# Moving the sums of the other rows behind the last expert's last bias, and one activation part ahead of one weight part, at the end of a mixture-of-experts kernel

## The chip, the cores and the metric

The kernel runs on one core of a Trainium2 chip. The metric is the device time of one execution in microseconds; lower is better. The core has a matrix engine (PE, whose weight loads are listed as PEld), a vector engine (DVE), an activation engine (ACT), a general engine (POOL) and a queue engine (SP) that here only issues transfers. Each engine takes its instructions strictly in the order in which the program lists them for it, so an instruction that waits holds back everything that is listed behind it on the same engine.

## The reference

One layer over 512 latent tokens of width 1024: a modulated norm, a mixer (a chunked scan with a convolution, and a pooling group), an output projection, a second modulated norm, a router that takes the best 4 of 32 experts for each token, the experts, and a last norm. Only the end matters here:

```
hb  = x_pad[toks] @ w1[e] + b1[e]
act = min(hb[::2], 7) * sigmoid(1.702 * min(hb[::2], 7)) * (clip(hb[1::2], -7, 7) + 1)
y   = (act @ w2[e] + b2[e]) * gate
x   = x + g2 * sum of y over the token's four experts
out = x * rsqrt(mean(x * x) + 1e-6) * final_norm_w
```

All inputs are 32-bit floats. The last line needs the complete sum of a token's row, so no row of the output can be made before the last expert that the row uses has been added.

## The kernel before, in words

Every 32-bit product is made of parts: an operand is split into a high part, which ACT copies out in a reduced format (fp32r), and a low part, which DVE makes by subtraction. PE then multiplies the pairs that matter and adds them up in its accumulators.

The 32 experts are worked one after the other, sorted by how many tokens they have. The late positions of the order, and the last one among them, have room for 64 tokens (the case `m == LT` in the code; `LT = 64`). For these the high and low activations lie side by side as one 128-column operand, so that the low products come out in the lower 64 accumulator rows; `rest` (L1321) copies those rows by ACT into the lower half of `b2h`, and the bias product `bias2` (L1339) adds them to the upper ones together with the bias.

The second layer of an expert reads its weights in four pieces of 1 MB, `kk` = 0 to 3 (L1672). Each piece is split by `split` (L1088): the high part on ACT (L1093), the low part on DVE (L1094). There are three pairs of buffers for high and low parts, so a piece waits until PE is done with the piece three before it. PE multiplies the activations with them in `prod` (L1347, matmuls on L1353), eight matmuls to a piece for the last expert. The activations come from `transposed` (L1122): PE transposes, ACT copies the high part (L1129), DVE subtracts the low part (L1130).

When an expert is done, `finish` (L1370) multiplies its rows by gate and `g2` (two DVE instructions, L1374) and adds them to `acc_scr`, an array in HBM, by an indirect transfer that POOL issues (L1376). The last expert's rows are not waited for in that way. Its output rows are added on chip instead: the four 128-row chunks of `acc_scr`, without the last expert, are read back by four transfers of 512 KB (L1683, `tot`), after the scatter of the expert before it has landed. The function `others` (L1685) brings one chunk into PE's accumulators, by a product with the identity: chunk 0 whole in 32 bits (`WHOLE = (0,)`; PE runs it in two passes for each half, which the trace lists as four matmuls), chunks 1 to 3 as a high part (ACT, L1690) and a low part (POOL for 1 and 3, DVE for 2, L1693), four matmuls each (L1697). Then the last expert's rows (`y`, split into `yh` by ACT on L1708 and `yl` by DVE on L1709) are put to their tokens by products with a 0/1 matrix `place` (L1716), 16 matmuls that contract over 64 rows only, four to a chunk and in the order of the chunks. From the finished sums ACT takes squares (L1728), DVE and POOL make the factor (L1730, L1731), DVE scales (L1734), and SP writes the chunk out (L1735).

In the program text the chunks 0 to 2 of `others` stand behind the four pieces and before `rest`, `bias2` and `finish`; chunk 3 stands behind `yh` and `yl` (`LATE_HI = 1`), and its high part is also held behind the last `yh` on ACT.

The order of the instructions on each engine is not the order of the text. A planner walks through the program with its own costs for each operation and lists, for each engine, what by its reckoning is ready first, the earlier in the text ahead where several are. `after(i, j, why)` (L1386) puts an instruction `i` behind `j`, in that list, without a semaphore where both are on one engine.

Of the kernel before, what the change touches and what calls it, by code (L numbers as in the profile page):

```python
# [5 lines left out]
F32 = mybir.dt.float32  # L6
# [5 lines left out]
ALU = mybir.AluOpType  # L12
# [9 lines left out]
NT = T // P  # L22
# [12 lines left out]
E = 32  # L35
# [62 lines left out]
def mixer_and_moe(tc, a):  # L98
    nc = tc.nc
    SC, VE, PO, PE, SP = nc.scalar, nc.vector, nc.gpsimd, nc.tensor, nc.sync  # L100
# [135 lines left out]
    for k in range(KT):  # L236
        for h in range(2):
            r = raw_tile([P, D])
            wdma = SP.dma_start(r, wm[:, k, h * D:(h + 1) * D])
            hi, lo = split_weights(r, [P, D])  # L240
            for i, w in enumerate((hi, lo)):
                for j in range(2):
                    last = PE.matmul(modp[2 * h + j][0:4, :], lhsT=sil4[:, k, :], rhs=w[:, j * T:(j + 1) * T],
                                     start=(k == 0 and i == 0), stop=(k == KT - 1 and i == 1))
            with tc.issue_after(wdma.ins):
                if 2 * k + h in (5, 9):
                    j = k // 2 - 1
# [4 lines left out]
    ahead = []  # L252
# [22 lines left out]
    then = [[(con[:, P:], con_src[:, P:])], [scan_con], [pool_con, (pw, a["pool_w"].rearrange("o g i f -> i (o g) f"))]]  # L275
# [13 lines left out]
    for j in range(16):  # L289
# [8 lines left out]
                            op0=ALU.add, op1=ALU.mult)  # L298
# [11 lines left out]
    for lo, n, which, oh_, ol_ in ((NT, NTC, 1, hch, hcl), (0, NT, 0, hxh, hxl)):  # L310
        for k in range(KT):
            tp = bank("S")
            w = n * P
            for j in range(n):
# [3 lines left out]
                             op0=ALU.mult, op1=ALU.add)  # L318
            SC.activation(row_of(oh_, k), val[:, 0:w], AF.Copy)
            (PO if k % 3 == 2 else VE).tensor_tensor(row_of(ol_, k), val[:, 0:w], row_of(oh_, k).bitcast(F32),  # L320
                                                     op=ALU.subtract)
# [166 lines left out]
    for xh_, xl_, n, off in ((hch, hcl, TC, T), (hxh, hxl, T, 0)):  # L488
        dps = bank("S")
        o = dps[0:2 * H, 0:n]  # L490
# [210 lines left out]
    sums = {}  # L701
# [104 lines left out]
    for pr in range(2):  # L806
        cath, catl = cat[pr]
        for k2 in range(6):
            tp = bank("S")
            for i in range(2):  # L810
                kk = 2 * k2 + i
# [3 lines left out]
            for i in range(2):  # L815
                kk = 2 * k2 + i
# [4 lines left out]
                                        op0=ALU.mult, op1=ALU.subtract)  # L821
# [220 lines left out]
    b2h = pc.tile([P, D], F32R, name="b2h")  # L1042
# [19 lines left out]
    newest_lo = [None]  # L1062
    loads = [0]
    own = [(strm, SR)]
    ring = [(pcat, RC)] * 3 + [(strm, SR)] * SR + [(pcat, RC)] * (RC - 3)
# [50 lines left out]
    def gather(t, col, m):  # L1116
# [2 lines left out]
                              bounds_check=T - 1, oob_is_err=False)  # L1119
        return t  # L1120

    def transposed(src, m, pool, name, bufs, tbank):  # L1122
        if m == LT:
            both = pool.tile([P, KT, 2, LT], F32R, name=name + "h", tag=name + "h", bufs=bufs)
            tp = tbank()
            for k in range(KT):
                PE.transpose(tp[:, k * LT:(k + 1) * LT], src[0:LT, k * P:(k + 1) * P], ident[0:LT, 0:LT])  # L1127
            v = tp.rearrange("p (k t) -> p k t", k=KT)
            SC.activation(both[:, :, 0, :], v, AF.Copy)  # L1129
            VE.tensor_tensor(both[:, :, 1, :], v, both[:, :, 0, :].bitcast(F32), op=ALU.subtract)  # L1130
            return (both.rearrange("p k i t -> p k (i t)"),)
        hi = pool.tile([P, KT, P], F32R, name=name + "h", tag=name + "h", bufs=bufs)
        lo = pool.tile([P, KT, P], F32R, name=name + "l", tag=name + "l", bufs=bufs)
        for h in range(2):
            tp = tbank()
            for k in range(4):
                PE.transpose(tp[:, k * P:k * P + m], src[0:m, (h * 4 + k) * P:(h * 4 + k + 1) * P],
                             ident[0:m, 0:m])
            o = hi[:, h * 4:(h + 1) * 4, 0:m]
            v = tp.rearrange("p (k t) -> p k t", k=4)[:, :, 0:m]  # L1140
            SC.activation(o, v, AF.Copy)
            VE.tensor_tensor(lo[:, h * 4:(h + 1) * 4, 0:m], v, o.bitcast(F32), op=ALU.subtract)
        return hi, lo


    slt = pc.tile([P, 4, LT], F32R, name="slt")
# [3 lines left out]
    sel2 = []  # L1150
# [15 lines left out]
    xgs = [pc.tile([P, D], F32, name=f"xg{i}") for i in range(2)]  # L1166
    for t in xgs:
        PO.memset(t, 0.0)
    lead = []
# [25 lines left out]
    for pr in range(2):  # L1195
        cs_ = (2 * pr, 2 * pr + 1)
        op = out_proj(pr, ks[4 * (pr == 0):], 2)
        for c in cs_:
            for h in range(2):
                hs = slice(h * T, (h + 1) * T)  # L1200
                VE.tensor_tensor(op[c, h], op[c, h], g1[:, hs], op=ALU.mult)
                VE.tensor_tensor(x1[c][:, hs], x1[c][:, hs], op[c, h], op=ALU.add)
        for c in cs_:
# [3 lines left out]

    psa = moe(tc, a, c_, cst, psa, psb, phx, pc, pd, g2, b1h, b2h, msum[:, NT - 1, :], top4, tab, first[0], table_out,
              acc_scr, halfneg, ring, ring_raw, ring_load, ring_split, w1_piece, w1_pair, w2_pair, gather, transposed, xgs,
              lead, slt, sel2)  # L1210
    pc.release()
    phx.release()
    pcat.release()
# [13 lines left out]
LATE_HI = 1  # L1227
# [26 lines left out]


def moe(tc, a, c_, cst, psa, psb, phx, pc, pd, g2, b1h, b2h, msum, top4, tab, last, table_out, acc_scr, halfneg,
        ring, raw, load, split, w1_piece, w1_pair, w2_pair, gather_, transposed_, xgs, lead, slt, sel2):
    nc = tc.nc
    SC, VE, PO, PE, SP = nc.scalar, nc.vector, nc.gpsimd, nc.tensor, nc.sync
    ident = c_("ident")  # L1260
# [43 lines left out]
    B1, B2, REST = (0, 2), 1, 3  # L1304
# [34 lines left out]
    def bias2(banks, m, sl):  # L1339
        for j, bk in enumerate(banks):  # L1340
            js = slice(j * 512, (j + 1) * 512)
            if m == LT:
                PE.matmul(bk[0:m, :], lhsT=slt[:, B2, :], rhs=b2h[:, js], start=False, stop=True, skip_group_check=True)
            else:
                PE.matmul(bk[0:m, :], lhsT=sl[0:2 * E, 0:m], rhs=b2h[0:2 * E, js], start=False, stop=True)

    def prod(banks, m, x, k, hi, lo, last=False):  # L1347

# [7 lines left out]
    def swiglu(t, m, out, plus=0.0):  # L1356
# [10 lines left out]
            VE.tensor_scalar(u, v[:, :, 1], 1.0 + LIMIT, 1.0 - LIMIT, op0=ALU.min, op1=ALU.max)  # L1367
        VE.scalar_tensor_tensor(out[0:m, :], g, GLIMIT, u, op0=ALU.min, op1=ALU.mult)

    def finish(banks, m, gcol, icol):  # L1370
        y = phx.tile([P, D], F32, name="y", bufs=2)
        for h in range(2):
            hs = slice(h * 512, (h + 1) * 512)
            VE.scalar_tensor_tensor(y[0:m, hs], banks[h][0:m, :], gcol[0:m, :], g2[0:m, hs],  # L1374
                                    op0=ALU.mult, op1=ALU.mult)
        PO.indirect_dma_start(out=acc_scr, out_offset=bass.IndirectOffsetOnAxis(ap=icol[0:m, :], axis=0),  # L1376
                              in_=y[0:m, :], in_offset=None, bounds_check=T - 1, oob_is_err=False,
                              compute_op=ALU.add)
        return y
# [6 lines left out]
    def after(i, j, why):  # L1386
        tc.add_manual_dep(i.ins, j.ins.name, mybir.DependencyInfo(
            mybir.DependencyClass.NoSync, mybir.DependencyReason.DATA), reason=why)
# [184 lines left out]
    for p in range(E):  # L1573
        e = ids[p] = expert(p)
        m = CAPS[p][0]
        if p != MID:
            x = nxt
# [95 lines left out]
    for kk in range(KT // 2):  # L1673
        hi, lo = split(load(w2_pair(ids[p], kk)))
        for i in range(2):
            prod(bk, m, act, 2 * kk + i, hi[:, i * D:(i + 1) * D], lo[:, i * D:(i + 1) * D])
        if kk == 0:
            end()

    tot, sums = [], []  # L1680
    for c in range(NT):
        tot.append(half())
        SP.dma_start(tot[c], acc_scr[c * P:(c + 1) * P, :])  # L1683

    def others(c):  # L1685
        sums.append(halves(bank("B")) if c < 2 else [bank("C") for _ in range(2)])
        parts = [(ident, tot[c])]
        if c not in WHOLE:
            hi, lo = [half(F32R) for _ in range(2)]
            x = SC.activation(hi, tot[c], AF.Copy)  # L1690
            if c >= NT - LATE_HI:
                after(x, last, "the last rows go ahead")
            (PO if c in TOTP else VE).tensor_tensor(lo, tot[c], hi.bitcast(F32), op=ALU.subtract)  # L1693
            parts = [(unit, hi), (unit, lo)]
        for j in range(2):
            for i, (u, v) in enumerate(parts):
                PE.matmul(sums[c][j], lhsT=u, rhs=v[:, j * 512:(j + 1) * 512], start=(i == 0), stop=False)  # L1697

    for c in range(NT - LATE_HI):
        others(c)  # L1700
    if m == LT:
        rest(bk)
    bias2(bk, m, sl)
    y = finish(bk, m, gcol, icol)
    yh, yl = [half(F32R) for _ in range(2)]
    for j in range(2):
# [104 lines left out]
```

## Time and profile before

| | |
|---|---|
| Time, median of 3 runs | 1791.74 us (1791.06 to 1792.96) |
| The profiled execution's own time | 1794.53 us |
| Its span in the profile | 1792.7 us |
| PE busy | 1640.6 us (92%) |
| DVE busy | 1526.3 us (85%) |
| ACT busy | 1170.2 us (65%) |
| POOL busy | 596.2 us (33%) |
| Mean clock granted to PE | 0.966 of full speed |

All starts below are microseconds from the start of this span. A row of the timeline gives start, duration, engine, line, operation, output, input and shapes; the number in square brackets is how long the engine had been idle before it and what ended that. A row of the table of stretches gives a stretch, its length, the busy time of each engine in it with the number of instructions, the clock that PE was granted as a share of full speed, and what the transfers did. A row of the chain of waits gives a start, a duration and the instruction or transfer that was the last thing waited for.

### The profile page before, as it was taken

The page shows a single profiled execution, that of the slowest core. Times are in us where ns is not written, and L with a number is a line of the kernel's source. Part 1 is how long each engine was busy: PE and PEld are TensorE (multiplying, and loading weights), DVE is VectorE, ACT ScalarE, POOL GpSimd, SP SyncE. Part 2 cuts the span into 40 slices and gives each one's busy share as a digit, 9 for nine tenths or more (in the row PEclk, how much of TensorE's full clock was granted, in tenths as well). Part 3 has the DMA queues.
Part 4 walks back from the last instruction along what each step waited for, and adds up shares of the span by engine and source line. Part 5 has one row for each costly group of instructions (what it writes and reads, how often), then busy time and mean ns, then how long its engine had stood idle before and what let it go on. Part 6 is the DMA issues. An engine that isn't in the chain of part 4 may idle for free. (4 is left out here: it accounts for less than half of the span.)

```text
span 1792.7 us, 21257 instructions
## 1 busy us (share of the span) xinstructions
PE 1640.6 (92%) x7311; PEld 1203.0 (67%) x7311; DVE 1526.3 (85%) x1486; ACT 1170.2 (65%) x1207; POOL 596.2 (33%) x287
## 2 busy tenths in 40 slices
PE   6999889998899899999999999999999998999985
PEld 2777667776778677767766667766666666666653
DVE  7768888987777899899999999976799999999993
ACT  6445436556643577687777777755678787777772
POOL 1203456779210011152041440502063362322302
PEclk9989999999999899999999999999999999999996
DMA  9646443223568789999999999976899999999952
GB/s 352 198 126 214 152 153 114 92 83 113 194 221 325 290 329 365 377 380 382 377 370 379 377 381 390 353 298 202 339 370 388 388 365 372 384 373 377 382 207 103
DMA packets 138417, 521.44 MB, mean 291 GB/s; under 512 B 14798, under 2 KB 44942, under 8 KB 106560
## 3 DMA queue, kind: packets, MB, share of 16 engines
q1 hardware_dynamic: 125446, 490.39, 72.1%
q0 software_dynamic: 6736, 16.70, 4.0%
q10 hardware_dynamic: 6122, 12.94, 2.2%
q8 instruction: 59, 0.97, 0.2%
q14 instruction: 54, 0.44, 0.1%
HBM read 508.26 MB, written 18.37 MB: 294 GB/s over the span
## 5 line engine op out<-in xcount | busy, mean ns | idle before, releaser
L1094 DVE TENSOR_TENSOR lo<-raw,hi 128x2048 fp32r<-128x2048 f32 x398 | 896.9, 2283 | 88.8 <-ACT hi L1093 86.2
L1093 ACT ACTIVATE hi<-raw 128x2048 fp32r<-128x2048 f32 x398 | 751.8, 1915 | 183.8 <-PE A L1353 112.8
L1376 POOL DMA_INDIRECT acc_scr<-y,ixi x32 | 220.7, 6896 | 549.4 <-DVE y L1374 445.3
L1353 PE MATMUL A<-lo,xh 128*128 128x512 f32 (+3 forms) x1072 | 314.0, 410 | 32.6 <-DVE lo L1094 28.7
L1353 PE MATMUL A<-hi,xh 128*128 128x512 f32 (+3 forms) x1072 | 308.5, 404 | 11.5 <-ACT hi L1093 6.9
L1353 PEld LDWEIGHTS A<-lo,xh 128*128 128x128 f32 (+3 forms) x1072 | 187.1, 183 | 120.7 <-DVE lo L1094 72.1
L1353 PEld LDWEIGHTS A<-hi,xh 128*128 128x128 f32 (+3 forms) x1072 | 193.9, 184 | 69.7 <-ACT hi L1093 9.6
L1117 POOL DMA_INDIRECT xg<-h_scr,ixi x30 | 114.3, 3810 | 259.6 <-PE S L1127 175.3
L1353 PE MATMUL S<-lo,ah 128*128 128x512 f32 (+3 forms) x512 | 165.3, 404 | 15.2 <-DVE lo L1094 15.1
L1353 PE MATMUL S<-hi,ah 128*128 128x512 f32 (+3 forms) x512 | 164.6, 402 | 3.9 <-DVE ah L1130 3.9
L1353 PE MATMUL A<-hi,xl 128*128 128x512 f32 (+3 forms) x544 | 155.7, 399 | 0.0
L1353 PEld LDWEIGHTS S<-lo,ah 128*128 128x128 f32 (+3 forms) x512 | 90.3, 183 | 49.9 <-DVE lo L1094 24.3
L1353 PEld LDWEIGHTS A<-hi,xl 128*128 128x128 f32 (+3 forms) x544 | 96.0, 177 | 32.1
L1353 PEld LDWEIGHTS S<-hi,ah 128*128 128x128 f32 (+3 forms) x512 | 92.5, 184 | 33.8 <-DVE ah L1130 4.0
L228 ACT ACTIVATE hi<-raw 128x1024 fp32r<-128x1024 f32 (+1 forms) x73 | 75.9, 1045 | 38.8 <-PE A L355 13.4
L231 DVE TENSOR_TENSOR lo<-raw,hi 128x1024 fp32r<-128x1024 f32 (+1 forms) x59 | 77.1, 1311 | 17.7 <-ACT hi L228 17.0
L1353 PE MATMUL S<-hi,al 128*128 128x512 f32 (+3 forms) x272 | 85.6, 396 | 0.0
L630 ACT ACTIVATE row<-row,nb 128x128 f32<-128x128 f32 x192 | 59.5, 390 | 37.4 <-POOL row L626 37.4
L336 PE MATMUL A<-hx,hi 128*128 128x512 f32 x160 | 66.5, 416 | 3.5 <-DVE at L378 2.1
L338 PE MATMUL A<-hx,lo 128*128 128x512 f32 x160 | 66.4, 415 | 0.0
L337 PE MATMUL A<-hx,hi 128*128 128x512 f32 x160 | 65.6, 410 | 0.0
L378 DVE SCALAR_TENSOR_TENSOR at<-A,cw,at 128x510 f32<-128x510 f32 (+1 forms) x80 | 57.9, 740 | 7.2 <-ACT at L374 6.6
(464 smaller groups left out, 2457.9 us busy)
## 6 DMA issues: line engine op xcount, KB each, us to landing
raw<-in_w_dram SPq DMA_DIRECT2D x384, 1024.0 KB
raw<-in_w_in_dram SPq DMA_DIRECT2D x36, 512.0 KB
mraw<-in_w_mod_dram SPq DMA_DIRECT2D x32, 512.0 KB
raw<-in_w_out_dram SPq DMA_DIRECT2D x14, 1024.0 KB
row<-cs_scr ACTq DMA_DIRECT2D x32, 384.0 KB
raw<-in_w_mod_dram SPq DMA_DIRECT2D x16, 512.0 KB
raw<-in_w_in_dram SPq DMA_DIRECT2D x16, 384.0 KB
xt<-in_x_dram SPq DMA_DIRECT2D x4, 512.0 KB
```

The costliest lines, as they stand in the source:

```text
L228: SC.activation(hi, r, AF.Copy)
L231: e.tensor_tensor(lo, r, hi.bitcast(F32), op=ALU.subtract)
L336: PE.matmul(lat, lhsT=hi[:, k, :], rhs=row_of(hxh, k), start=(k == 0), stop=False)
L337: PE.matmul(lat, lhsT=hi[:, k, :], rhs=row_of(hxl, k), start=False, stop=False)
L338: newest[0] = PE.matmul(lat, lhsT=lo[:, k, :], rhs=row_of(hxh, k), start=False, stop=(k == KT - 1))
L378: VE.scalar_tensor_tensor(ac[:, u:v], src[:, u + o:v + o], cw[:, j, ct:ct + 1], ac[:, u:v], op0=ALU.mult, op1=ALU.add)
L630: SC.activation(row[:, h, :], row[:, h, :], AF.Exp, bias=nb[:, c, i:i + 1])
L1093: ia = SC.activation(hi, r, AF.Copy)
L1094: i = VE.tensor_tensor(lo, r, hi.bitcast(F32), op=ALU.subtract)
L1117: PO.indirect_dma_start(out=t[0:m, :], out_offset=None, in_=h2_scr, in_offset=bass.IndirectOffsetOnAxis(ap=col[0:m, :], axis=0), bounds_ch ...
L1353: PE.matmul(bk[0:n, :], lhsT=u[:, k, 0:n], rhs=v[:, j * 512:(j + 1) * 512], start=(k == 0 and i == 0), stop=((last or m == LT and k == KT ...
L1376: PO.indirect_dma_start(out=acc_scr, out_offset=bass.IndirectOffsetOnAxis(ap=icol[0:m, :], axis=0), in_=y[0:m, :], in_offset=None, bounds_ ...
```

## The change

Three things are edited.

First, `others` for chunks 0 to 2 stands behind `bias2` in the text, and each of its matmuls (two for chunk 0, four each for chunks 1 and 2) is put behind the last matmul of `bias2` on PE. Only the matmuls get this order: the high parts on ACT and the low parts on POOL and DVE do not.

Second, the low part of weight piece 1 of the last expert's second layer (DVE) is put behind the low part of the last expert's activations (DVE, L1130).

Third, the same low part is put behind the last DVE instruction of `finish` of the expert before (L1374).

Nothing is computed that was not computed before, no size and no buffer changes, and no transfer is added or taken away.

```
-            VE.tensor_tensor(lo[:, h * 4:(h + 1) * 4, 0:m], v, o.bitcast(F32), op=ALU.subtract)
+            newest_part[0] = VE.tensor_tensor(lo[:, h * 4:(h + 1) * 4, 0:m], v, o.bitcast(F32), op=ALU.subtract)
...
-            VE.scalar_tensor_tensor(y[0:m, hs], banks[h][0:m, :], gcol[0:m, :], g2[0:m, hs],
-                                    op0=ALU.mult, op1=ALU.mult)
+            newest_y[0] = VE.scalar_tensor_tensor(y[0:m, hs], banks[h][0:m, :], gcol[0:m, :], g2[0:m, hs],
+                                                  op0=ALU.mult, op1=ALU.mult)
...
         if kk == 0:
             end()
+        if kk == 1:
+
+            after(newest_lo[0], newest_part[0], "the activations go ahead")
+            after(newest_lo[0], newest_y[0], "the rows go ahead")
...
-    def others(c):
+    def others(c, then=None):
...
         for j in range(2):
             for i, (u, v) in enumerate(parts):
-                PE.matmul(sums[c][j], lhsT=u, rhs=v[:, j * 512:(j + 1) * 512], start=(i == 0), stop=False)
-
-    for c in range(NT - LATE_HI):
-        others(c)
+                x = PE.matmul(sums[c][j], lhsT=u, rhs=v[:, j * 512:(j + 1) * 512], start=(i == 0), stop=False)
+                if then is not None:
+                    after(x, then, "the last expert goes ahead")
+
     if m == LT:
         rest(bk)
-    bias2(bk, m, sl)
+    x = bias2(bk, m, sl)
+    for c in range(NT - LATE_HI):
+        others(c, x)
     y = finish(bk, m, gcol, icol)
```

`bias2` now returns its last matmul; `newest_lo` is the low part that `split` made last (L1095), handed into the function.

More of the change, by code (lines that the diff above doesn't have):

```diff
@@ L1120, in gather @@
         return t
+    newest_part = [None]
     def transposed(src, m, pool, name, bufs, tbank):
@@ L1129, in transposed @@
             SC.activation(both[:, :, 0, :], v, AF.Copy)
-            VE.tensor_tensor(both[:, :, 1, :], v, both[:, :, 0, :].bitcast(F32), op=ALU.subtract)
+            newest_part[0] = VE.tensor_tensor(both[:, :, 1, :], v, both[:, :, 0, :].bitcast(F32), op=ALU.subtract)
             return (both.rearrange("p k i t -> p k (i t)"),)
@@ L1209, in mixer_and_moe @@
               acc_scr, halfneg, ring, ring_raw, ring_load, ring_split, w1_piece, w1_pair, w2_pair, gather, transposed, xgs,
-              lead, slt, sel2)
+              lead, slt, sel2, newest_lo, newest_part)
     pc.release()
@@ L1256, in moe @@
 def moe(tc, a, c_, cst, psa, psb, phx, pc, pd, g2, b1h, b2h, msum, top4, tab, last, table_out, acc_scr, halfneg,
-        ring, raw, load, split, w1_piece, w1_pair, w2_pair, gather_, transposed_, xgs, lead, slt, sel2):
+        ring, raw, load, split, w1_piece, w1_pair, w2_pair, gather_, transposed_, xgs, lead, slt, sel2, newest_lo, newest_part):
     nc = tc.nc
@@ L1342, in bias2 @@
             if m == LT:
-                PE.matmul(bk[0:m, :], lhsT=slt[:, B2, :], rhs=b2h[:, js], start=False, stop=True, skip_group_check=True)
-            else:
-                PE.matmul(bk[0:m, :], lhsT=sl[0:2 * E, 0:m], rhs=b2h[0:2 * E, js], start=False, stop=True)
+                x = PE.matmul(bk[0:m, :], lhsT=slt[:, B2, :], rhs=b2h[:, js], start=False, stop=True,
+                              skip_group_check=True)
+            else:
+                x = PE.matmul(bk[0:m, :], lhsT=sl[0:2 * E, 0:m], rhs=b2h[0:2 * E, js], start=False, stop=True)
+        return x
     def prod(banks, m, x, k, hi, lo, last=False):
@@ L1368, in swiglu @@
         VE.scalar_tensor_tensor(out[0:m, :], g, GLIMIT, u, op0=ALU.min, op1=ALU.mult)
+    newest_y = [None]
     def finish(banks, m, gcol, icol):
```

## The prediction

> **What bounds the kernel now.** Everything that the change touches lies in the last 50 us, so I read the chain of waits there, then the timeline of each engine, then a table of stretches for PE's clock. First the chain:
>
> ```profile
> 1746.21 9.61 DMA acc_scr<-y,ixi
> ...
> 1755.88 3.51 DMA raw<-acc_scr
> ...
> 1759.53 3.61 PE A L1697 x4
> 1763.14 0.46 PE S L1353 x2
> 1763.60 0.23 PE A L1697
> 1763.83 1.37 PE S L1353 x6
> ...
> 1769.24 3.16 PE A L1716 x7
> 1772.40 1.71 PE S L1716 x4
> 1774.11 2.00 PE S L1697 x4
> 1776.11 2.02 PE S L1716 x4
> ...
> 1781.02 0.65 DVE raw L1734
> ```
>
> The scatter of expert 30's rows lands at 1755.82, the first chunk read back at 1759.39. Only then does PE run chunk 0's sums (L1697), and behind them the last eight matmuls of the last expert's second layer (L1353), which do not need these rows. PE's list simply has them in that order. The timeline of DVE shows what stands before and after:
>
> ```profile
> 1744.54 1.40 DVE L1374 SCALAR_TENSOR_TENSOR y<-S,gtp,g 80x512 f32<-80x512 f32 x2
> 1745.86 2.27 DVE L1094 TENSOR_TENSOR lo<-raw,hi 128x2048 fp32r<-128x2048 f32 x1
> 1748.06 0.68 DVE L1130 TENSOR_TENSOR ah<-S,ah 128x512 fp32r<-128x512 f32 x1
> 1748.66 2.27 DVE L1094 TENSOR_TENSOR lo<-raw,hi 128x2048 fp32r<-128x2048 f32 x1
> 1753.38 2.29 DVE L1094 TENSOR_TENSOR lo<-raw,hi 128x2048 fp32r<-128x2048 f32 x1 [2.44 <-ACT hi L1093]
> 1763.13 2.27 DVE L1693 TENSOR_TENSOR raw<-raw 128x1024 fp32r<-128x1024 f32 x1 [7.46 <-ACT raw L1690]
> 1767.07 1.40 DVE L1374 SCALAR_TENSOR_TENSOR y<-S,gtp,g 64x512 f32<-64x512 f32 x2 [1.67 <-PE S L1343]
> 1768.50 1.34 DVE L1709 TENSOR_TENSOR raw<-y,raw 64x512 fp32r<-64x512 f32 x2
> ```
>
> On ACT, in the same stretch, and PE's first matmul of that layer:
>
> ```profile
> 1744.98 0.60 ACT L1129 ACTIVATE ah<-S 128x512 fp32r<-128x512 f32 x1 [2.19 <-PE S L1127]
> 1745.47 1.90 ACT L1093 ACTIVATE hi<-raw 128x2048 fp32r<-128x2048 f32 x1
> 1751.43 1.92 ACT L1093 ACTIVATE hi<-raw 128x2048 fp32r<-128x2048 f32 x1 [4.06 <-PE S L1353]
> 1760.79 1.06 ACT L1690 ACTIVATE raw<-raw 128x1024 fp32r<-128x1024 f32 x1 [7.44 <-DMA raw<-acc_scr]
> 1762.04 1.06 ACT L1690 ACTIVATE raw<-raw 128x1024 fp32r<-128x1024 f32 x1 [0.19 <-DMA raw<-acc_scr]
> 1765.00 1.08 ACT L1327 ACTIVATE b2h<-S 64x512 fp32r<-64x512 f32 x2 [1.90 <-PE S L1353]
> 1767.84 1.29 ACT L1708 ACTIVATE raw<-y 64x512 fp32r<-64x512 f32 x2 [1.76 <-DVE y L1374]
> ```
>
> ```profile
> 1748.79 0.90 PE L1353 MATMUL S<-hi,ah 128*128 128x512 f32 x2 [3.85 <-DVE ah L1130]
> ```
>
> The last expert's second layer starts at 1748.79, 3.85 us late, for want of the activations' low part. The order on ACT is the other thing to see: both high parts of the rows read back (L1690, chunks 1 and 2) stand ahead of `rest` (L1327), and on DVE chunk 2's low part (L1693, ended 1765.40) stands ahead of the last expert's rows (L1374). The clock, in stretches cut where it steps:
>
> ```profile
> 1745.68:1749.10 3.42, 0.31 (x1) 0.30 (x2) 3.42 (x4) 1.69 (x1) 2.88 (x1) 1.00 0.00 0
> 1749.10:1752.52 3.42, 3.42 (x10) 2.61 (x9) 1.84 (x1) 1.09 (x1) 3.12 (x1) 0.52 0.00 0
> 1759.36:1762.78 3.42, 3.25 (x5) 1.51 (x5) 0.00 (x0) 1.79 (x2) 0.85 (x1) 0.51 0.94 381
> 1766.20:1769.62 3.42, 1.93 (x8) 0.91 (x6) 2.52 (x4) 1.75 (x3) 0.88 (x1) 1.00 0.00 0
> 1769.62:1773.04 3.42, 3.42 (x9) 2.46 (x8) 1.06 (x2) 1.95 (x6) 3.31 (x3) 0.51 0.19 24
> 1773.04:1776.46 3.42, 3.42 (x8) 1.91 (x7) 2.35 (x5) 2.20 (x8) 1.08 (x2) 0.50 0.00 0
> ```
>
> They are 3.42 us long (some between are left out). After a stretch with PE busy 0.31 or 1.93 us the clock is half, after one with 3.42 or 3.25 us of 128-row matmuls it is full again. Two stretches with PE busy throughout but mostly on the 64-row matmuls of L1716 (1769.62 to 1776.46) did not raise it. A matmul of 512 columns costs 0.23 us at full clock (1.37 for 6) and 0.50 at half (2.00 for 4).
>
> **The activations' low part, part by part.** It may start when `ah`'s high part is there (1745.58) and DVE is done with expert 30's rows (1745.94), instead of 1748.06: 2.1 us earlier. PE starts piece 0 at about 1746.65. Weight piece 1's low part moves to 1746.62, done at 1748.9; piece 0 takes 8 x 0.23 = 1.84 at full clock, to 1748.5, so PE waits 0.4 for it. Pieces 2 and 3 go through the same DVE: low part 2 to 1751.2; high part 3 starts when piece 0 is released (1748.5, 2.9 earlier) and is there at 1750.4; low part 3 then runs from 1751.2 to 1753.5, PE ends piece 3 some 1.4 later, at about 1755. Behind the delayed low part on DVE stand only those low parts; nothing else waits. Expert 30's rows stay first on DVE, so their scatter (POOL, 1746.21) and the read back (SP) keep their times. If the planner put the activations' part between or ahead of the two row instructions, scatter and read back would come up to 0.68 later, and so would the end; I take 0 and keep 0.68 for the range.
>
> **The sums behind the last bias.** Removed is the wait of the last eight matmuls for the read back: they end at about 1755 instead of 1765.20, 10 us earlier. That is not the gain, because `rest` follows on ACT, and ACT's list is not edited. Its two high parts wait for the read back and end at 1761.85 and 1763.10. With both ahead, `rest` runs from 1763.12 to 1764.2, against 1765.00 to 1766.08 before: 1.9 us, out of 10. The first bias matmul can follow its half of `rest` at 1763.7, the second ends at about 1764.8 at half clock. On DVE chunk 2's low part holds the rows until 1765.40, so `y` runs 1765.40 to 1766.80 (before 1767.07), `yh` and `yl` as before behind it, done by 1768.2.
>
> What moves in between on PE is the price. The sums (four recorded for chunk 0, which takes two passes, and eight for chunks 1 and 2) had filled waits before; now they stand between bias and `place`. PE has been idle from 1755 to 1763.7, so they start at half clock at 1764.8. Chunk 0 costs 3.61 there, to 1768.4. With the clock raised at the step of this profile, 1769.7, two and a half of the other eight run at 0.50, the rest at 0.23: to 1770.95. Then place for chunks 0 to 2 is 12 x 0.23 = 2.8, to 1773.7; chunk 3's low part is ready by then (`yh` ends 1767.5, its high part 1768.6, the scatter 1.73 and the subtract 2.66 on POOL in turn from 1767.07: 1771.5); its sums and place are 8 x 0.23 = 1.84: last matmul 1775.5 against 1778.13. POOL's rows:
>
> ```profile
> 1761.93 2.38 POOL L1693 TENSOR_TENSOR raw<-raw 128x1024 fp32r<-128x1024 f32 x1 [9.71 <-DMA raw<-acc_scr]
> 1768.74 1.73 POOL L1376 DMA_INDIRECT acc_scr<-y,ixi  x1 [4.43 <-DVE y L1374]
> 1770.23 2.66 POOL L1693 TENSOR_TENSOR raw<-raw 128x1024 fp32r<-128x1024 f32 x1
> ```
>
> From the last matmul to the end of the last scaling are 1778.13 to 1781.67, and after it the output and the closing; these I leave as they are. So 2.6 us are gained with the clock steps where the profile has them. The gain is: wait removed 2.3 on the rows, sums moved in front of place (they start it 2.4 later than 1768.52), tail at full instead of half clock, some 4 to 5.
>
> The steps of the clock are not tied to the kernel's start, so the raise may come anywhere from 3.4 to 6.8 us after PE's steady work begins at 1763.7. Raised at 1767.1 or before, all is worth 4.3 (sums to 1769.2, last matmul 1773.8); raised at 1770.5, 1.8. The middle is 3.0, which I take. A wait of POOL's low part 1 (to 1764.31) lies under chunk 0's sums. What no row shows is whether 64-row matmuls hold a clock that is already full. If they do not, it falls at the step after 1773.04 and the last ten matmuls cost 0.50 instead of 0.23: 2.7 back, gain about 0 (rival 4 below). With full-row sums in the same stretches I expect it to hold.
>
> The two stretches from 1769.62 show PE busy for 6.8 us at 0.51 and 0.50 of full speed, and the fall at 1769.62 came with no gap of PE over 1.3 us before it. [...]
>
> **The rivals.** (1) `rest` gets between the two high parts on ACT, since piece 3 is earlier in the planner's reckoning too. For it: the planner had chunk 0's sums ahead of piece 3's first matmuls and chunk 2's behind its last, so chunk 2's rows come only a little before `rest` by its costs. Against: the added order gives it at most one low part (2.27) to gain. Then `rest` is 1761.87 to 1762.95, `y` 1763.6 to 1765.0, sums from 1763.9, clock up at 1766.3, last matmul about 1773.2: gain 4.9, 1786.8.
>
> (2) `rest` goes ahead of both. Then the last expert's `yh` and `yl` are done at about 1759.3, and the end is bound by the read back: high part 3 to 1764.2, POOL's low part 1, scatter and low part 3 to 1768.7, eight matmuls at 0.23 to 0.50: 1770.5 to 1772.7. Gain 5.4 to 7.6, say 6.5: 1785.2. Against it: in the chain a sum of chunk 1 (1763.60) stands between the matmuls of piece 3, so its high part was early by the planner's costs.
>
> (3) Slower: the pile behind the bias stays at half clock. Its place is PE from 1764.8; its price is 3.6 + 8 x 0.50 = 7.6 to 1772.4, 12 place at 0.45 to 0.50 to 1778.1, and 4.0 for chunk 3: 1782.1, 4.0 us later: 1795.7. It decides when no stretch after 1764.8 raises the clock. Against: 1759.36 to 1762.78 raised it with just these sums.
>
> (4) Nothing is left: the clock is raised among the sums and lost again at 1773.04, because place contracts over 64 rows; the sum above then ends at 1775.5 + 2.7 = 1778.2, where it ended before: 1791.7. For it speaks that two stretches of such work did not raise the clock; against it, that holding is not raising, and four of the last ten matmuls are full-row sums.
>
> **How the numbers follow.** The profiled execution took 1794.53 with a span of 1792.7, 2.8 above the median of the runs shown; the sum is a difference, and I put it on the median: 1791.74 - 3.0 = 1788.7. Its chance is 0.52, its own range 1787.0 to 1791.7. Rival 1 has 0.17, rival 2 0.12, rival 3 0.09, rival 4 0.10. A measurement of this kernel can tell about 0.2% (3.6 us) from no change. Faster by more than that: rivals 1 and 2 and a third of my case, 0.46. Slower by more: most of rival 3, 0.08. Within: 0.46. The range reaches past the middle of rival 2 (1785.2) and, at the other end, 0.7 for a late scatter and a little of rival 3 over rival 4's 1791.7; it leaves out most of rival 3 and the faster half of rival 2: 1784.4 to 1792.6.
>
> **What would show it.** PE's first matmul of the last expert's second layer near 1746.7 and piece 3 over by 1756 show the second and third edit right. `rest` starting at 1763, not 1756, shows that ACT holds it; a start at 1756 makes my forecast wrong and rival 2 right. The sums in one block behind L1343, at half clock first, show the price; L1716 at 0.23 shows the tail's gain, at 0.5 rival 3. A scatter later than 1746.2 would show expert 30's rows held back.

## Result and the profile after

| | before | after |
|---|---|---|
| Time, median of 5 runs each, taken in turn on one chip | 1792.96 us (1791.06 to 1794.93) | 1783.98 us (1781.36 to 1787.61) |
| Ratio, with its 95% interval | | 0.995 (0.9937 to 0.9964) |
| Same comparison again, median of 5 runs of the changed kernel (e5 below) | 1793.74 us | 1787.58 us, ratio 0.9964 (0.9951 to 0.9976) |
| The profiled execution's own time, its span | 1794.53, 1792.7 us | 1785.24, 1783.4 us |

The change is faster by 0.4 to 0.5%, some 6 to 9 us, where 3.0 were predicted. The median lies 0.4 us below the predicted range (1784.4 to 1792.6) and that of the repeat inside it, so what has to be explained is less the size than where the gain comes from. The two profiled executions are not level when the end begins: expert 30's rows start on DVE at 1744.54 before and at 1742.43 after, although the lists up to there are the same. From those rows to the end of the span it is 48.2 us before (1792.7 - 1744.54) and 41.0 after. So the profiles show 7.2 us from the changed stretch, and the other 2.1 are drift ahead of it. All comparisons of places below are made from those rows, or from the scatter behind them.

First the chain of waits of the changed kernel (start, duration, what was waited for):

```profile
1744.10 4.73 DMA acc_scr<-y,ixi
...
1749.29 4.41 DMA raw<-acc_scr
...
1753.72 1.06 ACT raw L1700
...
1754.80 0.60 ACT b2h L1329
...
1755.93 0.44 PE S L1345
...
1756.37 3.02 PE A L1707 x5
...
1762.67 1.66 PE A L1728 x7
...
1767.93 0.55 DVE raw L1746
...
1768.59 2.06 DVE raw L1746 x3
...
1772.54 0.25 DVE raw L1746
```

The first line is the surprise: the scatter of expert 30's rows has landed 4.73 us after its issue, against 9.61 before. The timelines of POOL, DVE, ACT and PE of the changed kernel show how:

```profile
1744.10 1.41 POOL L1382 DMA_INDIRECT acc_scr<-y,ixi  x1 [31.97 <-DVE y L1380]
```

```profile
1742.43 1.39 DVE L1380 SCALAR_TENSOR_TENSOR y<-S,gtp,g 80x512 f32<-80x512 f32 x2
1743.75 0.67 DVE L1132 TENSOR_TENSOR ah<-S,ah 128x512 fp32r<-128x512 f32 x1
1744.35 6.68 DVE L1094 TENSOR_TENSOR lo<-raw,hi 128x2048 fp32r<-128x2048 f32 x3
1755.93 1.40 DVE L1380 SCALAR_TENSOR_TENSOR y<-S,gtp,g 64x512 f32<-64x512 f32 x2 [4.91 <-PE S L1345]
1757.26 1.21 DVE L1703 TENSOR_TENSOR raw<-raw 128x1024 fp32r<-128x1024 f32 x1
```

```profile
1753.72 1.06 ACT L1700 ACTIVATE raw<-raw 128x1024 fp32r<-128x1024 f32 x1 [5.62 <-DMA raw<-acc_scr]
1754.80 1.08 ACT L1329 ACTIVATE b2h<-S 64x512 fp32r<-64x512 f32 x2
1755.90 1.06 ACT L1700 ACTIVATE raw<-raw 128x1024 fp32r<-128x1024 f32 x1
```

```profile
1744.48 0.73 PE L1357 MATMUL S<-hi,ah 128*128 128x512 f32 x2 [1.65 <-DVE ah L1132]
...
1752.13 0.62 PE L1357 MATMUL S<-lo,ah 128*128 128x512 f32 x2
```

POOL is busy with the scatter for 1.41 us, where it was 6.01 before:

```profile
1746.21 6.01 POOL L1376 DMA_INDIRECT acc_scr<-y,ixi  x1 [31.97 <-DVE y L1374]
```

DVE's list differs from the one before in two places of this stretch: the activations' low part stands ahead of the weights' low parts, and the last expert's rows (L1380) stand ahead of chunk 2's low part (L1703), which had held them back before. On ACT `rest` (L1329) stands between the two high parts (L1700), the order of rival 1.

### The profile page after: what moved, and what is told of

It is laid out like the page before. It is cut to its first block, busy times and chain, and to the rows that moved or that the text cites. A ratio compares the mean times of both kernels' runs of the same rounds, so it can differ in the third digit from the quotient of the medians.

```text
span 1783.4 us, 21256 instructions
## 1 busy us (share of the span) xinstructions
PE 1634.9 (92%) x7311; PEld 1199.5 (67%) x7311; DVE 1524.0 (85%) x1486; ACT 1170.2 (66%) x1207; POOL 594.1 (33%) x287
## 5 line engine op out<-in xcount | busy, mean ns | idle before, releaser
L1382 POOL DMA_INDIRECT acc_scr<-y,ixi x32 | 216.7, 6773 | 544.8 <-DVE y L1380 444.6
L228 ACT ACTIVATE hi<-raw 128x1024 fp32r<-128x1024 f32 (+1 forms) x73 | 76.0, 1045 | 39.0 <-PE A L355 10.8
```

The lines of the kernel that those rows point to most:

```text
L228: SC.activation(hi, r, AF.Copy)
```

## Experiments

Since the end begins some us earlier or later from execution to execution (POOL's scatter starts between 1739.83 in e15 and 1749.10 in e9), the table counts the end in each profile from the start of POOL's scatter to the end of the span. For e11 to e18 the time is that of one execution, with the one of the kernel before on the same chip in brackets. The scatter's length is that of the one profiled execution in every line.

| run | scatter on POOL, us | scatter's start to end of span, us | time, us |
|---|---|---|---|
| before | 6.01 | 46.5 | 1792.96 |
| after | 1.41 | 39.3 | 1783.98 |
| e1_sums_only | 6.01 | 44.6 | 1793.61, ratio 1.0 (0.9991 to 1.0008) |
| e2_part_only | 1.41 | 38.3 | 1785.76, ratio 0.9962 (0.9950 to 0.9975) |
| e3_rest_first | 1.41 | 37.7 | 1787.09, ratio 0.9966 (0.9954 to 0.9979) |
| e4_gap | 6.61 | 46.9 | 1793.07, ratio 0.9995 (0.9985 to 1.0006) |
| e5_changed_again | 1.41 | 39.6 | 1787.58, ratio 0.9964 (0.9951 to 0.9976) |
| e6_gap_two | 6.61 | 46.9 | 1795.24, ratio 1.001 (1.0001 to 1.002) |
| e8_part_first | 7.61 | 46.1 | 1793.89, ratio 1.0002 (0.9992 to 1.0011) |
| e9_late2 | 1.41 | 36.4 | 1785.05, ratio 0.9948 (0.9934 to 0.9963) |
| e11_gap_after | 1.41 | 40.1 | 1786.05 (1795.19) |
| e12_twice | 1.41 | 41.4 | 1786.85 (1795.19) |
| e13_gap_waits_act | 6.61 | 46.9 | 1792.31 (1795.19) |
| e14_twice_80 | 6.61 | 45.4 | 1791.08 (1794.26) |
| e15_twice_g2 | 1.41 | 40.8 | 1782.47 (1794.26) |
| e16_twice_flat | 1.41 | 40.5 | 1786.72 (1794.26) |
| e17_twice_96 | 6.61 | 47.2 | 1796.16 (1794.07) |
| e18_twice_112 | 3.81 | 43.9 | 1793.10 (1794.07) |

Seventeen of these eighteen lines fall into two groups: scatter 1.41 us and 36.4 to 41.4 us to the end, or scatter 6 us and more and 44.6 to 47.2. Only e18 lies between them in both. The kernel before belongs to the second group.

**The parts of the change.** e1 has the first edit alone, e2 the second and third alone.

```diff
 e1, against the changed kernel:
-        if kk == 1:
-            after(newest_lo[0], newest_part[0], "the activations go ahead")
-            after(newest_lo[0], newest_y[0], "the rows go ahead")
 e2, against the changed kernel:
+    for c in range(NT - LATE_HI):
+        others(c)
     if m == LT:
         rest(bk)
     x = bias2(bk, m, sl)
-    for c in range(NT - LATE_HI):
-        others(c, x)
```

> The first edit alone: the sums of chunks 0 to 2 stand behind the last bias product, DVE's order is that of before. Theory 1 (most of the gain comes from expert 30's scatter, whose issue on POOL took 6.0 us before and 1.4 after, and so from the rows being read back 4.9 us earlier): here the scatter takes 6.0 as before, ACT has both high parts ahead of the lower rows' copy, and the gain is the 1.8 to 4.3 us of the prediction's sum. Rival (most of the gain comes from the sums no longer standing in front of the last weight piece): 6 us or more faster than before.

> The second and third edit alone: the activations' low part ahead of the second weight low part, the sums where they were before. Theory 1: POOL issues expert 30's scatter in 1.4 us, the first chunk is back 4.9 us earlier, and as the chain of before hung on it, the time falls by 4 to 6 us. Rival: without the sums moved the last weight piece still stands behind chunk 0's sums on PE, so no more than 1 us is gained.

Moving the sums alone is worth nothing that can be measured (ratio 1.0, so within 1.6 us either way), and the activations' part alone gives all of it: e2 saves 7.9 us and e5, the whole change again, 6.2, with overlapping intervals. In e1 ACT has both high parts ahead of `rest`, as the prediction had assumed for the whole change. The timeline of PE in e1:

```profile
1761.74 1.17 PE L1345 MATMUL S<-b2h,slt 128*64 128x512 f32 x2 [4.72 <-ACT b2h L1329]
1762.71 3.62 PE L1703 MATMUL A<-raw,con 128*128 128x512 f32 x4
1765.34 1.94 PE L1703 MATMUL A<-raw 128*128 128x512 f32 x4
1767.12 1.08 PE L1703 MATMUL S<-raw 128*128 128x512 f32 x4
1768.13 2.12 PE L1724 MATMUL A<-raw 64*128 64x512 f32 x8
```

The price is as foreseen: the sums pile up behind the bias, chunk 0 (the first four) at half clock (0.50 from 1762.40 to 1765.80). The last matmul of e1's profile ends 30.9 us after expert 30's rows begin (1773.43 - 1742.51), against 33.6 before: 2.7 us earlier, where the prediction's sum gives 2.6. Of this 1.9 us reach the end of the span (46.5 - 44.6), and the runs show no gain. Why the medians show less than the profile stays open.

**`rest` ahead of both high parts, and one chunk less ahead of the rows.** e3 puts `rest` first on ACT, and e9 also leaves chunk 2 to the end (`LATE_HI = 2`).

```diff
 e3 and e9, against the changed kernel:
-    if m == LT:
-        rest(bk)
+    r = rest(bk)
 ... in others, for the chunks that are not late, x being the high part on ACT:
+                after(x, r, "the last expert's lower rows go ahead")
 e9 alone:
-LATE_HI = 1
+LATE_HI = 2
```

> The changed kernel with one more order: on ACT the lower rows' copy goes ahead of the high parts of chunks 1 and 2. Theory 1 together with the chain of the changed kernel (first high part, then the copy at 1754.80, while piece 3 was done at 1752.6): the bias product comes 2 us earlier, PE's gap in front of it shrinks from 2.7 us to about 0.7, the clock stays full for the sums, and the time falls 2 to 4 us below the changed kernel, 11 to 13 below before. Rival: POOL's low parts and the last chunk bind the end, 0 to 1 us below the changed kernel.

> The changed kernel with the lower rows' copy ahead of the high parts on ACT, as tried before, and chunk 2 too behind the last expert's rows (two late chunks instead of one), so that the rows' low part no longer waits on DVE for chunk 2. The run before had rows at 1757.3 but their low part only at 1762.2, behind chunk 2's. Expected: 1 to 3 us below the changed kernel; if the read back and POOL's low parts bind the end, no difference within 1 us.

e3 brings nothing: `rest` is not what ends last any more. Its chain of waits is bound by the read back of a later chunk, behind which stand that chunk's high and low part:

```profile
1752.14 6.50 DMA raw<-acc_scr
...
1758.65 1.06 ACT raw L1701
...
1759.74 1.24 DVE raw L1706
```

e9 takes that away, and has the shortest end in its profile (36.4 us). Its median is 2.5 us below the changed kernel's in the same set of runs, but the intervals overlap; it is the best of the kernels run here by a margin that these runs don't settle.

**Is it the scatter, or PE's earlier start?** e8 has the order of the changed kernel except that one of the two row instructions of expert 30 stands behind the activations' part.

```diff
 e8, against the changed kernel (newest_y[1] is the first row instruction):
+            after(newest_y[1], newest_part[0], "the rows go behind")
```

> The changed kernel with the activations' low part ahead of one of the two DVE instructions that make expert 30's rows, so that the last of them is followed directly by the weight low parts, and the scatter starts while such a low part runs. If the gain hangs on the scatter: POOL holds it until the three low parts are over, 7 to 8 us instead of 1.4, and the time is that of before or up to 1 us more, although PE starts the last expert's second layer as early as in the changed kernel. If the early start of that layer is what gains, it stays 4 us or more below before.

The timelines of DVE and POOL in e8:

```profile
1747.02 0.69 DVE L1132 TENSOR_TENSOR ah<-S,ah 128x512 fp32r<-128x512 f32 x1
1747.63 0.74 DVE L1381 SCALAR_TENSOR_TENSOR y<-S,gtp,g 80x512 f32<-80x512 f32 x1
1748.29 6.68 DVE L1094 TENSOR_TENSOR lo<-raw,hi 128x2048 fp32r<-128x2048 f32 x3
```

```profile
1748.65 7.61 POOL L1383 DMA_INDIRECT acc_scr<-y,ixi  x1 [32.96 <-DVE y L1381]
```

The activations' part is still ahead of these three weight low parts and PE starts early (at 1747.77, 1.6 us after expert 30's rows begin, against 4.25 before), but POOL takes the scatter up inside a weight low part and is not done until 1756.26, 1.29 us after DVE's three low parts end (1754.97). The whole gain is gone (ratio 1.0002). So the gain hangs on the early scatter, and the earlier start of PE is worth nothing that can be measured without it.

**What lets the scatter through?** In every profile in which it takes 6 us or more it ends 1.28 to 1.30 us after DVE falls idle (before: at 1752.22, DVE idle from 1750.93). A first theory was that DVE's weight low parts, which read two operands on chip, keep POOL out, and any instruction that reads the accumulators gives it an opening. e4 and e6 test it: the order of before, and between expert 30's rows and weight piece 1's low part one more DVE instruction of the same length. In e4 it multiplies the old accumulators by 1.0 in place, in e6 it subtracts a piece of `g2` from them into a free buffer; nothing reads either result.

```diff
 e4, e6, against the kernel before (names shortened; old: the accumulators of expert 30; after both stand the same two lines):
+            gap = VE.tensor_scalar(old, old, 1.0, None, op0=ALU.mult)                                  # e4
+            gap = VE.tensor_tensor(free, old, g2[0:80, 512:1024], op=ALU.subtract)                     # e6
+            after(gap, newest_y[0], "behind the rows")
+            after(newest_lo[0], gap, "the gap goes ahead")
```

> The kernel before, with one DVE instruction of 0.7 us added behind expert 30's rows and ahead of the second weight low part: it multiplies 80 rows of a used accumulator bank by 1 in place, and nothing reads them. Every other order is that of before. If POOL's scatter is held up by DVE's subtract of two operands in on-chip memory, which runs when the scatter starts, then an instruction that reads and writes an accumulator there lets it through: 1.4 us instead of 6.0, the first chunk back 4.9 us earlier, and the time 4 to 5 us lower, although DVE works 0.7 us more and the activations' low part comes 0.7 later. If the order of the activations' part is what matters, the scatter stays at 6.0 and the time is 0 to 1 us higher.

> As the kernel before with the added DVE instruction, but the instruction is now of the kind of the activations' low part: it subtracts an on-chip operand from the 80 rows of a used accumulator bank and writes the 80x512 result on chip, into a free buffer that nothing reads. The instruction before (one accumulator operand, in place) left the scatter at 6.6 us. If the kind of the DVE instruction that runs when POOL takes up the scatter decides, the scatter takes 1.4, the first chunk is back 4.9 earlier, and the time falls by 3.5 to 5, with nothing else moved. If something else in the changed order decides, the scatter stays above 6 and the time is that of before, within 1 us.

In both the scatter takes 6.61 us, 0.6 longer than before, by the length of the added instruction. From e4, the timelines of DVE and of POOL:

```profile
1743.44 0.68 DVE L1685 TENSOR_SCALAR S<-S 80x512 f32<-80x512 f32 x1
1744.04 2.27 DVE L1094 TENSOR_TENSOR lo<-raw,hi 128x2048 fp32r<-128x2048 f32 x1
1746.23 0.68 DVE L1130 TENSOR_TENSOR ah<-S,ah 128x512 fp32r<-128x512 f32 x1
1746.84 2.28 DVE L1094 TENSOR_TENSOR lo<-raw,hi 128x2048 fp32r<-128x2048 f32 x1
```

```profile
1743.79 6.61 POOL L1378 DMA_INDIRECT acc_scr<-y,ixi  x1 [31.98 <-DVE y L1376]
```

In this form, with an instruction over the 80 rows of expert 30, that theory fell. e5, the changed kernel again beside e6, made sure that its scatter is short each time:

> The changed kernel once more, beside the others of this set. It should be about 0.5% below before again; against the second and third edit alone (0.9962 in the set before) it tells what the moved sums add: 0 to 2 us.

Then the added instruction was brought nearer to the activations' part step by step. e12 puts an exact copy of it at that place, the real one being held behind weight piece 1's low part; e13 is e6 with a wait for ACT like the copy's; e11 is the changed kernel with e6's instruction ahead of the activations' part. e6, e12 and e13 have the same lists on every engine, except for what this one instruction reads and waits for.

```diff
 e12, against the kernel before (both: high and low activations; v: the accumulators that they are made from):
+                gap = VE.tensor_tensor(free[:, :, 1, :].bitcast(F32R), v, both[:, :, 0, :].bitcast(F32),
+                                       op=ALU.subtract)
             part = VE.tensor_tensor(both[:, :, 1, :], v, both[:, :, 0, :].bitcast(F32), op=ALU.subtract)
...
+            after(part, newest_lo[0], "behind the weights' low part")
 e14, e17, e18: the copy over rows 0:80, 0:96, 0:112
 e15: the copy with g2 as its on-chip operand; e16: as e15, in one run of 512 elements
```

> The changed kernel with the added subtraction of e6_gap_two between expert 30's rows and the activations' low part, so that POOL takes up the scatter during the added instruction and the activations' low part follows 0.6 us later, ahead of three weight low parts in a row. If the activations' low part lets a scatter in that is already waiting: scatter 1.4 to 2.1 us, time as the changed kernel plus 0.7. If the scatter has to meet it at the start: blocked until the weight low parts are over, 7 to 9 us, time as the kernel before.

> The order of the kernel before, with a copy of the activations' low part (same operands, same shape, same wait for ACT; its result is read by nothing) put on DVE between expert 30's rows and the low part of weight piece 1; the real one stays behind that low part. If something in that instruction or its wait lets the scatter through: scatter 1.4 us, its landing 4.7 to 4.9 us after the issue, sums and last bias some 4 us earlier, time 4 to 5 us below the kernel before. If only the real one's place or what PE does with it matters: scatter 6.6 us as in e4_gap and e6_gap_two, and the time of the kernel before within 0.2%.

> The kernel of e6_gap_two with the same lists on all engines, but the added subtraction of 80 rows also waits for ACT's high part of the activations, and so the low part of weight piece 1 behind it need not wait for ACT again. If the wait decides: scatter 1.4 us. If the operands or the shape decide: 6.6 us as in e6_gap_two while e12_twice shows 1.4. If neither shows 1.4, it is not the instruction between the rows and the weights' low part that decides.

From e12 and then from e13, the timelines of POOL and DVE:

```profile
1743.69 1.41 POOL L1385 DMA_INDIRECT acc_scr<-y,ixi  x1 [31.98 <-DVE y L1383]
```

```profile
1743.34 0.67 DVE L1134 TENSOR_TENSOR xg<-S,ah 128x512 fp32r<-128x512 f32 x1
1743.93 2.27 DVE L1093 TENSOR_TENSOR lo<-raw,hi 128x2048 fp32r<-128x2048 f32 x1
```

```profile
1743.50 6.61 POOL L1380 DMA_INDIRECT acc_scr<-y,ixi  x1 [31.98 <-DVE y L1378]
```

```profile
1743.14 0.67 DVE L1688 TENSOR_TENSOR xg<-S,g 80x512 fp32r<-80x512 f32 x1
1743.74 2.27 DVE L1094 TENSOR_TENSOR lo<-raw,hi 128x2048 fp32r<-128x2048 f32 x1
1745.94 0.68 DVE L1132 TENSOR_TENSOR ah<-S,ah 128x512 fp32r<-128x512 f32 x1
```

In both the scatter is taken up 0.35 to 0.36 us after the added instruction begins, and the weight low part follows 0.24 us later. With the copy it is through in 1.41 us; with the 80-row subtraction that waits for the same engine it takes 6.61. So neither the wait nor the place decides, and the earlier time of the real activations' part is not needed to let the scatter through: the copy alone, in the order of before, shortened the end from 46.5 to 41.4 us. e2, which has the earlier part as well, comes to 38.3. e11 shows that a scatter already waiting is let in too: taken up during the 80-row instruction, it ends at 1745.54, half a microsecond after the activations' part (1744.37 to 1745.04).

What is left between e12 and e13 is the number of partitions, the accumulators read, the on-chip operand and the pattern:

> The kernel of e12_twice with the copy of the activations' low part cut to 80 of its 128 partitions; lists, waits, operands and pattern are the same. If the number of partitions decides (e12_twice let the scatter through with 128, e13_gap_waits_act did not with 80): scatter 6.6 us. If not: 1.4 us.

> The kernel of e12_twice with g2 as the copy's on-chip operand in place of the activations' high part, read in the same 8 runs of 64, without the gaps between them; 128 partitions, same accumulator bank, same waits. If the operand decides: scatter 6.6 us. If not: 1.4 us.

> The kernel of e15_twice_g2 with all operands and the result as one run of 512 elements, as the 80-row subtraction of e13_gap_waits_act has them, but over 128 partitions. If the pattern of 8 runs decides: scatter 6.6 us while e15_twice_g2 shows 1.4. If not: the same as e15_twice_g2.

> The kernel of e14_twice_80 with the copy over 96 of the 128 partitions. If only an instruction over all 128 lets the scatter through: 6.6 us. If it is enough to reach past the 80 rows of the scatter: 1.4 us.

> The same with 112 of the 128 partitions: 6.6 us if all 128 are needed, 1.4 us if it is enough to reach past the 80 rows of the scatter, or if a bound lies between 96 and 112.

The operand and the pattern don't matter (e15, e16: 1.41). The number of partitions does: 80 and 96 keep the scatter out (e14, e17: 6.61), 112 let it through in part (3.81, neither of the two values expected), 128 wholly. e12 and e14 differ in nothing else, and the instruction takes 0.67 us in both. From e18, the timelines of POOL and DVE:

```profile
1747.45 3.81 POOL L1386 DMA_INDIRECT acc_scr<-y,ixi  x1 [31.98 <-DVE y L1384]
```

```profile
1747.10 0.67 DVE L1135 TENSOR_TENSOR xg<-S,ah 112x512 fp32r<-112x512 f32 x1
1747.70 2.27 DVE L1093 TENSOR_TENSOR lo<-raw,hi 128x2048 fp32r<-128x2048 f32 x1
1749.90 0.68 DVE L1137 TENSOR_TENSOR ah<-S,ah 128x512 fp32r<-128x512 f32 x1
```

With 112 partitions the scatter ended at 1751.26, 1.36 us after the next instruction over 128 partitions began (1749.90), and not, as all the others that were held up, after DVE's idle. The kernel before shows both outcomes, in the timelines of POOL and DVE:

```profile
1121.82 5.95 POOL L1376 DMA_INDIRECT acc_scr<-y,ixi  x1 [33.82 <-DVE y L1374]
...
1712.84 1.41 POOL L1376 DMA_INDIRECT acc_scr<-y,ixi  x1 [20.01 <-DVE y L1374]
```

```profile
1121.46 0.60 DVE L1142 TENSOR_TENSOR al<-S,ah 128x448 fp32r<-128x448 f32 x1
...
1126.40 1.27 DVE L1142 TENSOR_TENSOR xl<-S,xh 128x512 fp32r<-128x512 f32 x2
...
1712.49 0.47 DVE L1142 TENSOR_TENSOR al<-S,ah 128x320 fp32r<-128x320 f32 x1
```

The second is what the experiments give: an activations' part over 128 partitions right behind the rows, and 1.41 us. The first has the same thing behind rows of the same shape, and was held up for 5.95 all the same; it ended 1.37 us after the next two activations' parts in a row began (1126.40), with no idle time of DVE. Behind a low part the outcome varies too. The scatter of expert 30 in the kernel before was not let in by the part over 128 partitions at 1748.06, nor were those of e14 and e17 by the same instruction, while the one of e18 was; in e11, where that part came right behind the 80-row instruction, the waiting scatter was let in at once. So 128 partitions in the instruction that runs when POOL takes up the scatter were needed at the place tested, but are not always enough. Why the number of partitions matters, and what differs at 1121.82, stays open.

## Why the prediction was wrong, step by step

**The step that failed** is the sentence "Expert 30's rows stay first on DVE, so their scatter (POOL, 1746.21) and the read back (SP) keep their times". The scatter does start right behind the rows as before (1.67 us after their start in both profiles). But its length was taken as a property of the scatter, 9.61 us to the landing, and it is set by what DVE runs behind those rows (1.41 us on POOL in e12, 6.61 in e14). Landed after 4.73 us instead of 9.61, it takes 4.9 us out of the chain, which the sum did not have. The kernel before held the hint: the same instruction on L1376 with 6.01 and with 1.41 us. The prediction took over the first (the start, 1746.21, and the landing after 9.61) and did not look for the reason of the difference.

**The activations' low part** was right. It starts 1.32 us after expert 30's rows begin, against 3.52 before: 2.2 earlier, predicted 2.1. PE's last expert starts 2.05 us after those rows, against 4.25, and piece 3 is over 10.3 us after them (1752.75 - 1742.43), predicted 10.5. But e8 shows that this is worth nothing measurable by itself.

**The order on ACT** came out as rival 1 had it. `rest` starts 12.4 us after the rows; the prediction's 1763.12 is 18.6 after them. Of the 6.2 between, 4.9 are the scatter and 1.25 the second high part, with its wait, that no longer stands ahead. By the prediction's own sign a start near 1756 was to speak for rival 2: counted from the rows in the kernel before, `rest` came at 1756.9. But it came there with one high part still ahead of it, by the early scatter, which the sign did not allow for. Rival 1 kept the old read back, and so its 1786.8 (a gain of 4.9) stays above the measured median too.

**The price of the sums behind the bias** was right: from the first sum to the last matmul it is 10.8 us in the changed kernel (1756.37 to 1767.21), predicted 10.7 (1764.8 to 1775.5). So was the sum with the read back as before: in e1's profile the last matmul ends 30.9 us after the rows begin, predicted 31.0 (1775.5 - 1744.54). As a time it was over-estimated all the same: predicted 1.8 to 4.3, measured by the runs of e1 as 0 within 1.6. That the forecast of a gain came out the right way is therefore in good part luck: the gain measured is not the one that was reckoned.

**The clock.** The table of stretches of the changed kernel (stretch, length, busy times of PE, PEld, DVE, ACT and POOL, clock):

```profile
1757.00:1760.40 3.40, 3.40 (x7) 2.00 (x6) 2.67 (x4) 1.94 (x3) 3.01 (x3) 0.51 0.10 10
1760.40:1763.80 3.40, 3.40 (x13) 2.08 (x12) 0.00 (x0) 0.16 (x1) 1.76 (x1) 0.99 0.10 15
1763.80:1767.20 3.40, 3.40 (x13) 1.90 (x12) 1.57 (x4) 3.40 (x13) 0.58 (x1) 1.00 0.00 0
```

The clock rises among the sums, from 0.51 to 0.99, and stays full (1.00) where most of the work is the 64-row products. So rivals 3 and 4 are out, and the open point of the prediction (whether those matmuls hold a full clock) is answered as it took it. The steps are 3.4 us or twice that apart in both profiles (1759.45, 1762.87 and 1769.69 before, 1757.07 and 1760.48 after), but do not come at the same times from the kernel's start, as the prediction had it; the raise came 5.0 us after PE's steady work began (1755.44 to 1760.48), inside its 3.4 to 6.8. One reading of the clock was too simple: of the two stretches said to be mostly 64-row matmuls, the second (1773.04 to 1776.46) has 2.07 us of full-row sums (L1697) and 1.49 of `place`. The clock was still 0.50 behind it (1776.46 to 1778.20), so these two stretches say less of 64-row work alone than the prediction had them say.

**"These I leave as they are"**, of the time behind the last matmul, was off by 2.0 us: from the last matmul to the end of the last scaling it is 5.6 us now (1767.21 to 1772.79), before 3.5 (1778.13 to 1781.67). PE gives up the four chunks faster than DVE scales them: ACT is done with the last squares at 1768.37, but DVE scales two chunks until 1770.65 before it turns to the last chunk's factor (L1742, 1770.57). So DVE's lines L1746 stand in the chain. The last matmul comes 8.8 us earlier by this count (24.8 against 33.6 from the rows), of which the span keeps 7.2.

## What to carry to other kernels

The length of an indirect transfer's issue on POOL was not its own here (1.41 to 22.66 us on the one line L1376 of the kernel before): look for the same line elsewhere in the trace, and where it takes several times as long in one place as in another, look at what DVE runs while POOL holds it. Here it paid to put a DVE instruction over all 128 partitions that reads the accumulators between the instruction that makes the rows and a run of instructions with two on-chip operands (e12: scatter 1.41 us against 6.01, and 41.4 us to the end of the span against 46.5). A prediction that keeps the time of a transfer should say what that time hangs on, and an order that is changed for one engine should be followed on the engines that wait for it.

## What the runs showed of the hardware that was not expected

At the place of the change, a scatter that POOL issued while DVE ran subtractions with two on-chip operands was held until 1.28 to 1.30 us after DVE fell idle, through several instructions in a row, for 6.0 to 7.6 us; e18 is the exception. Instructions of 0.67 us that read the accumulators did not open a way for it over 80 partitions (e4, e6, e13, e14) or 96 (e17), did in part over 112 (e18), and did over 128 (e12, e15, e16).

Elsewhere in the kernel before the same line was held for 14.81 us at 1678.02 and for 22.66 at 777.39. An idle DVE is not always what ends it: at 1121.82 the scatter got through at two activations' parts in a row, and at 1156.24, with 112 rows, at a single one over 128 partitions, 1.45 us after that began.

That the scatter waits for DVE, these traces show (6.01 against 1.41 us); by what it is kept out, no run here shows. In e4 it was taken up at 1743.79, during an instruction that reads and writes the accumulators alone (1743.44 to 1744.12), and was still kept out through it and three more, until 1750.40.

PE's clock stayed at 1.00 of full speed from 1763.80 to 1767.20 with eleven of thirteen matmuls over 64 rows, while in the kernel before 6.8 us of busy PE, 4.9 of them such matmuls, had not raised it from 0.5 (1769.62 to 1776.46).
